# The maximum of a row of attention scores taken in two pieces and joined

## The chip, the cores and the metric

The kernel runs on one core of one Trainium2 chip. The metric is the device time of one execution in microseconds (us), as the median of three runs. Everything below about where the time lies comes from one profiled execution.

## What is computed

A two-layer diffusion backbone over 1024 latent tokens and 256 context tokens, width 1024, in fp32. Layer 0 mixes grouped-query attention with a convolution module, layer 1 a long convolution with a recurrence, and each is followed by a gated feed-forward net. The change lies in the attention of layer 0. It has 12 query heads over 4 key/value heads of width 64; latent queries attend to context and latent keys (1280 keys), context queries to the context alone (256 keys):

```python
def one_block(q_blk):
    s = jnp.einsum('bqhgd,bkhd->bhgqk', q_blk, k).astype(jnp.float32)
    p = jax.nn.softmax(s, axis=-1).astype(v.dtype)
    return jnp.einsum('bhgqk,bkhd->bqhgd', p, v)
...
attn_l = block_attention(q_l, jnp.concatenate([k_c, k_l], axis=1), jnp.concatenate([v_c, v_l], axis=1))
```

The softmax subtracts the maximum of each row of scores before the exponential. That maximum is what the change computes in another way.

## The kernel before

The kernel has stages that follow one another: the input projections, the attention stage (with what is left of the convolution module's LayerNorm beside it), the output projection, the feed-forward net, then layer 1. The attention stage is `attention_all`. It works through 4 groups (one key/value head each) of 15 units. A unit is one query head with 256 queries: 12 units of a group are latent queries with 1280 keys ("full units", 48 in all), 3 are context queries with 256 keys ("context units", 12 in all). A unit holds its 256 queries as two halves, i = 0 and i = 1, of 128 rows each.

`score_steps` makes the scores of a unit. All scores lie in one PSUM tile `S` of 2560 columns: columns 0 to 1023 hold half 0 against the latents, 1024 to 1279 half 0 against the context, 1280 to 1535 half 1 against the context, 1536 to 2559 half 1 against the latents. Every score is the sum of two matmuls (L1009 and L1010, the keys' rounded part and rest). For half 0 there are four matmuls of 512 columns and then four of 256, which are the context scores of both halves. For half 1 there are four of 512. Then VectorE takes the row maximum over all 1280 columns, negated, into `nm` (L1026), and ScalarE takes the exponential of the whole row with `nm` as bias and sums it (L1027: the exponential and, as a second instruction, the readout of the sum).

`value_steps` multiplies with the values: for each of five blocks of 256 keys TensorE transposes four tiles of `p` into the PSUM tile `pT` (L1049, two buffers), ScalarE copies it rounded to `ph` (L1053), VectorE puts the rest into `pl` (L1054, which frees the buffer of `pT`), and TensorE adds four products into `o` (L1060). At a unit's end TensorE spreads the reciprocal of the sums (L1067), ScalarE copies half of `o` to `bot` (L1068), and VectorE joins and scales the result `ot` (two instructions that show as L1189, a helper's line). The reciprocal `rs` (L1041) waits for both exponentials of its unit.

`attention_all` interleaves the steps of the score and value generators by a list of due times, and the scheduler of the tile framework then sets each engine's final order. Each engine works its own queue strictly in that order. Pools are made with `reuse_waits="tile"`.

Of the kernel before, what the change touches and what calls it, by code (L numbers as in the profile page):

```python
# [10 lines left out]
F32 = mybir.dt.float32  # L11
F32R = mybir.dt.float32r
AF = mybir.ActivationFunctionType
ALU = mybir.AluOpType
AX = mybir.AxisListType
PSUM = bass.MemoryType.PSUM

P = 128
# [4 lines left out]
T = TC + TL  # L23
# [224 lines left out]
class Kern:  # L248
# [750 lines left out]
    def score_steps(self, u, state):  # L999

        nc = self.nc
        ab, S = self.ab, self.S
        nk, r, o, h0 = u
        q, k1, k2, vs = self.gr[h0 // 3]
        at = ((0, TL), (T + TC, T))

        def mm(i, dst, key, n):
            a = q[:, r, o + i * P:o + i * P + P]
            nc.tensor.matmul(S[:, dst:dst + n], lhsT=a, rhs=k1[:, key:key + n], start=True, stop=False)  # L1009
            nc.tensor.matmul(S[:, dst:dst + n], lhsT=a, rhs=k2[:, key:key + n], start=False, stop=True)  # L1010
        nm, sm = (ab.tile([P, 2], F32, name=m, tag=m, bufs=4) for m in ("nm", "sm"))
        state["p"], state["sm"] = [], sm
        for i in range(2):
            lo = at[i][1]
            if nk == T:
                lo = min(at[i])
                for n in range(0, TL, 512):
                    mm(i, at[i][0] + n, TC + n, 512)
                    if n == 0:
                        yield  # L1020
            if i == 0:
                for n in range(2):
                    mm(n, at[n][1], 0, TC)
            s = S[:, lo:lo + nk]
            p = ab.tile([P, T], F32, name="p", tag="p", bufs=self.npr)[:, :nk]
            nc.vector.tensor_reduce(out=nm[:, i:i + 1], in_=s, op=ALU.max, axis=AX.X, negate=True)  # L1026
            nc.scalar.activation(p, s, AF.Exp, bias=nm[:, i:i + 1], accum_out=sm[:, i:i + 1])  # L1027
            state["p"].append(p)
            yield
# [921 lines left out]
```

## Time and profile before

| | us |
|---|---|
| runs | 3836.53, 3836.60, 3843.24 (median 3836.6) |
| the profiled execution | 3845.4, of which the span 3843.6 |
| attention stage in it | about 391 to 978, of it the first group to about 554 |
| TensorE busy in 554 to 687 (12 full and 3 context units) | 108.8 of 133 |
| VectorE busy there | 91.9 of 133 |
| ScalarE busy there | 84.3 of 133 |

The span runs from the first to the last instruction. Busy time of TensorE is that of its matmuls; their weight loads are a line of their own (PEld) and lie beside them. A row of the timeline gives the start in us from the span's start, the duration, engine, line, operation, output and inputs; brackets at its end give idle time of the engine just before it and what ended it. Rows of equal instructions are merged, with their count.

### The profile page before, as it was taken

To read this page: it belongs to the slowest core of one execution; us is meant where nothing else is said; L and a number is where in the kernel's file an instruction comes from. 1 tells how busy PE (TensorE), PEld (TensorE's weight loads), DVE (VectorE), ACT (ScalarE), POOL (GpSimd) and SP (SyncE) were. 2 spreads that over 40 slices of the span, in tenths; PEclk is the share of its full clock that TensorE was granted. 3 is DMA by queue.
4 is the path that set the end of the run, shared out by engine and by line. 5 is a ranking of instruction groups with operands and counts; after the bars stand their busy time and mean duration, and the time that the engine had idled before them with its cause. 6 is when DMAs were issued, how large, how long until landed. Compare 5 with 4: busy or idle time off the path is not lost.

```text
span 3843.6 us, 47920 instructions
## 1 busy us (share of the span) xinstructions
PE 3509.9 (91%) x18708; PEld 2920.9 (76%) x18708; DVE 2295.9 (60%) x2884; ACT 1237.7 (32%) x2115; POOL 1323.9 (34%) x964
## 2 busy tenths in 40 slices
PE   7988788888899999999999899999787899999998
PEld 4768567666787888888888778977666778888886
DVE  5987566667226656645556688365697453443435
ACT  4134666665233111222222422222112332222222
POOL 3248131110262111223333554356566642222223
PEclk9999799999999999999999999999888999999999
DMA  5374111000322223212222467522346311111111
GB/s 205 117 193 107 43 56 32 21 30 14 106 83 93 83 88 106 68 60 71 76 76 74 142 200 200 152 85 96 117 138 209 115 55 50 50 45 50 43 51 55
DMA packets 202866, 351.12 MB, mean 91 GB/s; under 512 B 23504, under 2 KB 124432, under 8 KB 202640
## 3 DMA queue, kind: packets, MB, share of 16 engines
q1 hardware_dynamic: 172240, 311.22, 25.0%
q0 software_dynamic: 26496, 30.48, 3.7%
q10 hardware_dynamic: 3904, 6.36, 0.5%
q8 instruction: 148, 2.42, 0.3%
q14 instruction: 78, 0.64, 0.1%
HBM read 275.04 MB, written 62.39 MB: 88 GB/s over the span
## 4 chain that ended last, share of the span: by engine, by line
PE 67%; DVE 12%; issue 4%; ACT 3%; DMA 2%; POOL 2%; SPq 0%; POOLq 0%; DVEq 0%; ACTq 0%
PE dl L338 13%; PE dl L339 13%; PE dl L340 13%; PE pj L338 2%; PE pj L340 2%; PE pj L339 2%; DVE nm L1026 2%; PE pT L1049 2%; PE o L1060 2%; DVE pl L1054 2%; PE S L1009 1%; PE dc L338 1%; PE dc L340 1%; PE dc L339 1%; PE S L1010 1%
## 5 line engine op out<-in xcount | busy, mean ns | idle before, releaser
L332 POOL TENSOR_TENSOR wlo<-wraw,whi 128x1024 fp32r<-128x1024 f32 (+1 forms) x226 | 579.1, 2568 | 1284.3 <-ACT whi L331 1273.6
L339 PE MATMUL dl<-hl,whi 128*128 128x512 f32 x1920 | 762.6, 397 | 3.9 <-POOL hl L1189 3.2
L338 PE MATMUL dl<-hh,whi 128*128 128x512 f32 x1536 | 606.9, 396 | 7.2 <-DVE fc L1100 4.0
L340 PE MATMUL dl<-hh,wlo 128*128 128x512 f32 x1536 | 608.0, 396 | 0.0
L331 ACT CAST whi<-wraw 128x1024 fp32r<-128x1024 f32 (+1 forms) x226 | 224.9, 1004 | 875.2 <-PE dl L339 401.7
L339 PEld LDWEIGHTS dl<-hl,whi 128*128 128x128 f32 x1920 | 362.4, 189 | 87.8 <-POOL hl L1189 4.8
L1098 DVE SCALAR_TENSOR_TENSOR fc<-dl,cols,fc 128x1023 f32<-128x1023 f32 x84 | 107.4, 1279 | 409.5 <-ACT fc L1097 409.4
L338 PEld LDWEIGHTS dl<-hh,whi 128*128 128x128 f32 x1536 | 289.3, 188 | 76.0 <-ACT nt L486 3.6
L340 PEld LDWEIGHTS dl<-hh,wlo 128*128 128x128 f32 x1536 | 289.5, 188 | 68.8
L872 DVE SCALAR_TENSOR_TENSOR x<-dl,modT,x 128x1024 f32<-128x1024 f32 x160 | 204.2, 1278 | 115.6 <-PE dl L340 114.1
L338 PE MATMUL dl<-gs,whi 128*128 128x512 f32 x640 | 253.3, 396 | 9.2 <-DVE fc L1100 9.2
L339 PE MATMUL dl<-gs,whi 128*128 128x512 f32 x640 | 250.2, 391 | 0.0
L340 PE MATMUL dl<-gs,wlo 128*128 128x512 f32 x640 | 249.8, 390 | 0.0
L1054 DVE TENSOR_TENSOR pl<-pT,ph 128x512 fp32r<-128x512 f32 x252 | 167.7, 686 | 67.5 <-ACT ph L1053 66.9
L1049 PE MATMUL pT<-ident,p 128*128 128x128 f32 x1008 | 166.0, 287 | 44.2 <-DVE pl L1054 37.3
L1053 ACT CAST ph<-pT 128x512 fp32r<-128x512 f32 x252 | 142.2, 587 | 150.1 <-PE pT L1049 148.4
L1026 DVE TENSOR_REDUCE nm<-S 128x1 f32<-128x1280 f32 (+1 forms) x120 | 153.0, 1275 | 49.5 <-PE S L1010 44.7
L1060 PE MATMUL o<-ph,vs 128*128 128x256 f32 x504 | 146.7, 304 | 34.9 <-ACT ph L1053 17.5
L1193 DVE SCALAR_TENSOR_TENSOR conv<-u,cols,conv 128x1287 f32<-128x1287 f32 (+14 forms) x104 | 173.2, 1695 | 0.9
L1049 PEld LDWEIGHTS pT<-ident,p 128*128 128x128 f32 x1008 | 120.7, 145 | 66.8 <-DVE pl L1054 51.2
L338 PE MATMUL dl<-hl,whi 128*128 128x512 f32 x384 | 154.0, 402 | 2.0 <-ACT whi L331 0.9
L1060 PE MATMUL o<-pl,vs 128*128 128x256 f32 x504 | 152.8, 326 | 2.1 <-DVE pl L1054 2.1
(376 smaller groups left out, 8340.6 us busy)
## 6 DMA issues: line engine op xcount, KB each, us to landing
wraw<-in_wup SPq DMA_DIRECT2D x88, 512.0 KB, 3.6
adaw<-in_adaw SPq DMA_DIRECT2D x128, 256.0 KB, 2.9
wraw<-in_wdn SPq DMA_DIRECT2D x44, 512.0 KB, 3.6
adaw<-in_adaw SPq DMA_DIRECT2D x32, 512.0 KB, 4.4
df<-in_dftf POOLq DMA_DIRECT2D x64, 256.0 KB, 3.9
wraw<-in_w1f SPq DMA_DIRECT2D x24, 512.0 KB, 3.8
x<-in_xT SPq DMA_DIRECT2D x16, 640.0 KB, 9.8
spd<-so SPq DMA_DIRECT2D x68, 128.0 KB, 2.6
```

The costliest lines, as they stand in the source:

```text
L331: nc.scalar.copy(hi[:, :cols], raw[:, :cols])
L332: nc.gpsimd.tensor_tensor(out=lo[:, :cols], in0=raw[:, :cols], in1=hi[:, :cols].bitcast(F32), op=ALU.subtract)
L338: mm(out, lhsT=lh, rhs=rh, start=first, stop=False)
L339: mm(out, lhsT=lh, rhs=rl, start=False, stop=False)
L340: mm(out, lhsT=ll, rhs=rh, start=False, stop=last)
L872: nc.vector.scalar_tensor_tensor(out=xl, in0=pl, scalar=self.mod(l, j, m, 0), in1=xl, op0=ALU.mult, op1=ALU.add)
L1026: nc.vector.tensor_reduce(out=nm[:, i:i + 1], in_=s, op=ALU.max, axis=AX.X, negate=True)
L1049: nc.tensor.transpose(pt[:, (2 * a + i) * P:(2 * a + i + 1) * P], p[:, kc * P:(kc + 1) * P], self.ident)
L1053: nc.scalar.copy(ph, pt)
L1054: nc.vector.tensor_tensor(out=pl, in0=pt, in1=ph.bitcast(F32), op=ALU.subtract)
L1060: nc.tensor.matmul(o, lhsT=vs[:, kc], rhs=x[:, a * 256:a * 256 + 256], start=(kc == 0 and j == 0), stop=(kc == nk // P - 1 and j == 1))
L1193: self.nc.vector.scalar_tensor_tensor(out=out, in0=a, scalar=s, in1=b, op0=ALU.mult, op1=op)
```

## The change

For a full unit the maximum is no longer one reduction over 1280 columns. As soon as the first 512 latent columns of a half have been issued, a first reduction is issued over what is there: columns 0 to 511 for half 0, and 1280 to 2047 (768 columns, the context scores and the first latents) for half 1. When the rest has been issued a second reduction takes the remaining columns: 768 for half 0, 512 for half 1. Both write into a small tile `mx`, negated, and the smaller of the two goes into `nm`. Context units keep their single reduction (now L1033). Nothing else is edited; lines after it shift by seven.

```diff
                 for n in range(0, TL, 512):
                     mm(i, at[i][0] + n, TC + n, 512)
                     if n == 0:
+                        e = at[i][0] + 512
+                        mx = ab.tile([P, 2], F32, name="mx", tag="mx", bufs=4)
+                        nc.vector.tensor_reduce(out=mx[:, 0:1], in_=S[:, lo:e], op=ALU.max, axis=AX.X, negate=True)
                         yield
...
-            nc.vector.tensor_reduce(out=nm[:, i:i + 1], in_=s, op=ALU.max, axis=AX.X, negate=True)
+            if nk == T:
+                nc.vector.tensor_reduce(out=mx[:, 1:2], in_=S[:, e:lo + nk], op=ALU.max, axis=AX.X, negate=True)
+                nc.vector.tensor_tensor(out=nm[:, i:i + 1], in0=mx[:, 0:1], in1=mx[:, 1:2], op=ALU.min)
+            else:
+                nc.vector.tensor_reduce(out=nm[:, i:i + 1], in_=s, op=ALU.max, axis=AX.X, negate=True)
```

The scheduler gives another order around it. TensorE before, from the end of one full unit in the last group to the first transposes of the next (`k` are the two parts of the keys, `p` the exponentials; the names in brackets are the engines' semaphores that a row waits for):

```order
L1067 MATMUL o<-ident,rs 64x128 x2
L1009 MATMUL S<-k_6739,q 128x512 [waits Activation_49]
L1010 MATMUL S<-k_6740,q 128x512
L1009 MATMUL S<-k_6739,q 128x512
L1010 MATMUL S<-k_6740,q 128x512
L1009 MATMUL S<-k_6739,q 128x256
L1010 MATMUL S<-k_6740,q 128x256
L1009 MATMUL S<-k_6739,q 128x256
L1010 MATMUL S<-k_6740,q 128x256
L1049 MATMUL pT<-ident,p 128x128 x6
```

All eight score matmuls stand together, and only the first of them waits, for ScalarE. TensorE now, at the same place of another unit of the same group (L1074 is the old L1067, L1056 the old L1049, L1067 the old L1060):

```order
L1074 MATMUL o<-ident,rs 64x128 x2
L1009 MATMUL S<-k_6892,q 128x512 [waits Activation_49]
L1010 MATMUL S<-k_6893,q 128x512
L1056 MATMUL pT<-ident,p 128x128 x6
L1009 MATMUL S<-k_6892,q 128x512 [waits DVE_49]
L1010 MATMUL S<-k_6893,q 128x512
L1009 MATMUL S<-k_6892,q 128x256
L1010 MATMUL S<-k_6893,q 128x256
L1009 MATMUL S<-k_6892,q 128x256
L1010 MATMUL S<-k_6893,q 128x256
L1067 MATMUL o<-ph,vs 128x256 [waits Activation_49]
```

The first pair of scores has moved ahead of the transposes, and the second pair now waits for VectorE. In the built program the value that it waits for is the one that the first reduction of the same half sets, in all 96 halves of full units: the second pair writes the tile `S` that this reduction reads, and the wait is put on the tile as a whole, though the columns are others.

VectorE before, from the first half of a full unit to the end of the unit (`nm` once for each half):

```order
L1026 TENSOR_REDUCE nm<-S 128x1 [waits PE_49]
L1054 TENSOR_TENSOR pl<-pT,ph 128x512 [waits Activation_49] x3
L1054 TENSOR_TENSOR pl<-pT,ph 128x512 [waits DVE_49,Activation_49]
L1026 TENSOR_REDUCE nm<-S 128x1 [waits PE_49]
L1054 TENSOR_TENSOR pl<-pT,ph 128x512 [waits DVE_49,Activation_49]
L1041 RECIPROCAL rs<-sm 128x2 [waits Activation_49]
L1189 TENSOR_TENSOR ot<-o,bot 64x256 [waits DMAHW6_49,Activation_49]
L1189 TENSOR_TENSOR ot<-o,ot 64x256 [waits DVE_49]
```

VectorE now, over one full unit of the same group (L1061 is the old L1054, L1196 the old L1189):

```order
L1022 TENSOR_REDUCE mx<-S 128x1 [waits PE_49]
L1061 TENSOR_TENSOR pl<-pT,ph 128x512 [waits Activation_49] x2
L1030 TENSOR_REDUCE mx<-S 128x1 [waits PE_49]
L1031 TENSOR_TENSOR nm<-mx 128x1 [waits DVE_49]
L1061 TENSOR_TENSOR pl<-pT,ph 128x512 [waits Activation_49] x2
L1022 TENSOR_REDUCE mx<-S 128x1 [waits PE_49]
L1061 TENSOR_TENSOR pl<-pT,ph 128x512 [waits Activation_49]
L1030 TENSOR_REDUCE mx<-S 128x1 [waits PE_49]
L1031 TENSOR_TENSOR nm<-mx 128x1 [waits DVE_49]
L1196 TENSOR_TENSOR ot<-o,bot 64x256 [waits DMAHW2_49,Activation_49]
L1196 TENSOR_TENSOR ot<-o,ot 64x256 [waits DVE_49]
```

Each reduction has become two, with subtractions `pl` between them, and a joining instruction that waits for the second. Counted over the program, in the first half the two reductions have two `pl` between them in 45 of 48 full units, and in 11 a `pl` also stands ahead of the join; in the second half a `pl` stands between the reductions in 24 units, and in 8 the first instruction of `ot` stands there and both `pl` ahead of the first reduction.

## Prediction

> **What bounds the kernel now.** I read the page first, for the engines and the chain that ended last, then the busy time by stretches of the attention stage, then the timeline of one unit in it. From the page, the busiest engine and the chain by engine:
>
> ```profile
> PE 3509.9 (91%) x18708; PEld 2920.9 (76%) x18708; DVE 2295.9 (60%) x2884; ACT 1237.7 (32%) x2115; POOL 1323.9 (34%) x964
> ...
> PE 67%; DVE 12%; issue 4%; ACT 3%; DMA 2%; POOL 2%; SPq 0%; POOLq 0%; DVEq 0%; ACTq 0%
> ```
>
> TensorE carries two thirds of the chain over the whole span, so what is worth asking is whether it carries the attention stage too. Busy time by stretches (columns as in the header):
>
> ```profile
> core 0: us, PE busy (x) PEld busy (x) DVE busy (x) ACT busy (x) POOL busy (x), PEclk, DMA share, GB/s
> 391.00:554.00 163.00, 126.80 (x683) 102.80 (x684) 87.51 (x143) 102.74 (x183) 49.30 (x92) 0.81 0.16 51
> 554.00:687.00 133.00, 108.84 (x737) 92.26 (x734) 91.94 (x138) 84.32 (x162) 24.28 (x50) 0.99 0.10 29
> ```
>
> The second stretch is one group of 12 full and 3 context units in 133 us. No engine is full in it: TensorE 108.84, VectorE 91.94, ScalarE 84.32, and the durations of matmuls overlap, which makes TensorE's figure too high. So the group is held by a chain of waits between engines. The timeline of one full unit shows it (start, duration, engine, line, operation):
>
> ```profile
> 886.62 0.33 PE L1049 MATMUL pT<-ident,p 128*128 128x128 f32 x1 [0.56 <-DVE pl L1054]
> 887.14 0.38 PE L1067 MATMUL o<-ident,rs 128*64 128x128 f32 x2
> 887.23 0.19 ACT L1027 ACTIVATION_READ_ACCUMULATOR p<-S,nm 128x1 f32 x1
> 887.47 0.50 PE L1009 MATMUL S<-k,q 128*128 128x512 f32 x1
> 887.56 0.37 ACT L1068 COPY bot<-o 64x256 f32<-64x256 f32 x1
> 887.81 0.40 PE L1010 MATMUL S<-k,q 128*128 128x512 f32 x1
> 887.96 0.42 DVE L1189 TENSOR_TENSOR ot<-o,bot 64x256 f32<-64x256 f32 x1 [0.34 <-ACT bot L1068]
> 888.05 0.40 PE L1009 MATMUL S<-k,q 128*128 128x512 f32 x1
> ...
> 888.88 0.28 PE L1010 MATMUL S<-k,q 128*128 128x256 f32 x1
> 889.00 0.82 PE L1049 MATMUL pT<-ident,p 128*128 128x128 f32 x6
> 889.20 1.49 DVE L1026 TENSOR_REDUCE nm<-S 128x1 f32<-128x1280 f32 x1 [0.36 <-PE S L1010]
> 889.58 1.07 ACT L1053 CAST ph<-pT 128x512 fp32r<-128x512 f32 x2 [1.65 <-PE pT L1049]
> 890.60 1.28 DVE L1054 TENSOR_TENSOR pl<-pT,ph 128x512 fp32r<-128x512 f32 x2
> 890.72 1.33 ACT L1027 ACTIVATE p<-S,nm 128x1280 f32<-128x1280 f32 x1
> 891.95 0.19 ACT L1027 ACTIVATION_READ_ACCUMULATOR p<-S,nm 128x1 f32 x1
> ...
> 893.10 0.39 PE L1009 MATMUL S<-k,q 128*128 128x512 f32 x1
> 893.62 0.69 DVE L1054 TENSOR_TENSOR pl<-pT,ph 128x512 fp32r<-128x512 f32 x1 [0.22 <-ACT ph L1053]
> 893.80 0.40 PE L1010 MATMUL S<-k,q 128*128 128x512 f32 x1
> 894.23 1.49 DVE L1026 TENSOR_REDUCE nm<-S 128x1 f32<-128x1280 f32 x1
> 895.64 0.68 DVE L1054 TENSOR_TENSOR pl<-pT,ph 128x512 fp32r<-128x512 f32 x1
> ...
> 896.98 0.20 ACT L1027 ACTIVATION_READ_ACCUMULATOR p<-S,nm 128x1 f32 x1
> 897.23 0.50 PE L1009 MATMUL S<-k,q 128*128 128x512 f32 x1
> ```
>
> Follow the scores. Half 0 starts at 887.47, 0.05 after the readout of the exponential before it ended (887.23 + 0.19 = 887.42). Its last matmul ends at 889.16, the maximum starts at 889.20 and takes 1.49, the exponential starts at 890.72, its readout ends at 892.14. Half 1 starts at 893.10, its maximum at 894.23, its readout ends at 897.18, and at 897.23 the next unit's half 0 starts. Counted from 887.42 that is a closed ring of 9.76 us: half 0 ends at 4.72, half 1 at 9.76. It is closed because the first scores of a half wait for the exponential of the other half, although they go to other columns: the waits are for `S` as a whole. The only slack in the ring is the 0.96 between 892.14 and 893.10, in which TensorE worked through transposes queued ahead of half 1.
>
> **What the change costs, part by part.** VectorE's prices, from the groups of the stretch 391 to 985 (the number behind the bar is busy time, then the mean in ns):
>
> ```profile
> L1054 DVE TENSOR_TENSOR pl<-pT,ph 128x512 fp32r<-128x512 f32 x252 | 167.7, 686 | 67.5 <-ACT ph L1053 66.9
> L1026 DVE TENSOR_REDUCE nm<-S 128x1 f32<-128x1280 f32 x96 | 143.1, 1490 | 45.0 <-PE S L1010 43.6
> ...
> L1026 DVE TENSOR_REDUCE nm<-S 128x1 f32<-128x256 f32 x24 | 9.9, 414 | 4.5 <-ACT p L1027 3.2 <-PE S L1010 1.1
> L1041 DVE RECIPROCAL rs<-sm 128x2 f32<-128x2 f32 x60 | 9.9, 165 | 38.2 <-ACT p L1027 38.1
> ```
>
> A reduction of 1280 columns takes 1.490, one of 256 takes 0.414: 1.05 ns a column and 0.145 besides. So 512 columns cost 0.68 and 768 cost 0.95, both between measured rows. The join of two columns isn't in the trace; the reciprocal on 128x2 (0.165) is its nearest row and the lower end, the 256 column reduction (0.414) the upper; I take 0.16, as it has even less to do. A half so costs 0.68 + 0.95 + 0.16 = 1.79 instead of 1.49, over 96 halves 29 us more on VectorE. That alone is no loss in time, since VectorE idles 41 of 133.
>
> [...]
>
> What matters is the ring. The edit means the first reduction to run in the shadow of the second pair of scores. But the second pair now waits for the first reduction (the wait for VectorE in the order, for the whole tile). So nothing is overlapped: first pair, first reduction, second pair, second reduction, join, exponential, one behind the other. Besides, VectorE has subtractions queued between the two reductions, and TensorE's queue stands still behind the waiting pair: the products `o`, the transposes behind them, and the result of the unit before.
>
> Half 0, counted as above from the readout's end at 0:
> - First pair 0.05 to 0.79: two matmuls of 512 took 0.74 from start to end (887.47 to 887.81 + 0.40).
> - First reduction, 512 columns: 0.82 to 1.50.
> - Second pair and context scores: 1.55 to 2.76. In the trace such six took 1.11 (888.05 to 889.16); 0.10 more as they start from a stop, like the first one at 887.47.
> - Meanwhile six transposes go out at 0.63 (0.58 after the first matmul, as at 888.05). The copies `ph` start 0.58 after such transposes (889.00 to 889.58), so 1.21; the first is done at 1.80, and the pair of `pl` runs 1.82 to 3.10 (1.28, as at 890.60). It stands ahead of the second reduction, which could have started at 2.79.
> - Second reduction, 768 columns: 3.12 to 4.07. Join: 4.10 to 4.26. Exponential with readout, 1.42 (890.72 to 892.14): 4.29 to 5.71. Before: 4.72. Loss 0.99.
>
> Half 1:
> - First pair 5.76 to 6.50. The fourth `ph` is queued behind the exponential, 5.73 to 6.32, so its `pl` (0.69, as at 893.62), which stands ahead of the reduction, runs 6.34 to 7.03.
> - First reduction, 768 columns: 7.05 to 8.00. Second pair: 8.05 to 8.79. The last `pl` 8.02 to 8.71.
> - Second reduction, 512 columns: 8.82 to 9.50. Join 9.53 to 9.69.
> - The exponential stands behind the copy `bot` on ScalarE. `bot` waits for TensorE's last products, which wait for the last `pl`: from there to the end of L1067 is 0.90 (886.62 to 887.14 + 0.38), so 8.75 to 9.65, and `bot` (0.37) 9.69 to 10.06.
> - Exponential 10.08 to 11.51. The ring takes 11.51 instead of 9.76: a loss of 1.75 for a full unit; the old slack of 0.96 is eaten in it.
>
> In 8 units both `pl` stand ahead of the first reduction of half 1 and the first `ot` between the reductions: first reduction 7.76 to 8.71, second pair to 9.50; `ot` waits for `bot`, but by then has it (9.11 to 9.53); second reduction 9.55 to 10.23, second `ot` (0.42, as at 887.96) to 10.67, join to 10.86, exponential to 12.32. That is 0.81 more. In 11 units a `pl` of 0.69 stands ahead of the join of half 0.
>
> The sum: 48 x 1.75 + 8 x 0.81 + 11 x 0.69 = 84.0 + 6.5 + 7.6 = 98.1 us. The first group (163 us in the stretches above, other work in between) and the 12 full units beside context units are counted like the rest. What follows attention starts when it has ended, so the loss goes through: the profiled execution's 3845.4 would be 3943.5, and against the median of the runs, 3836.6, the forecast is 3934.7.
>
> **Rivals.**
> - *The wait doesn't hold anything up, and the change works as meant.* Then half 0 keeps its scores, and behind the last of them stand 0.95 + 0.03 + 0.16 = 1.14 instead of 1.49; half 1 has 0.87 instead of 1.49. That is 0.97 a unit or 47 us: 3790. It decides where the first reduction ends before TensorE reaches the second pair. For it: six transposes (0.66) stand between the pairs. Against: they are too short to cover 0.03 + 0.68 + 0.05, and in half 1 the reduction lasts 0.95 and starts late. Chance 0.06. [...]
> - *Only the bare ring grows*, because the subtractions give way (copies come earlier than I time them). Half 0: second reduction 2.80 to 3.75, exponential to 5.39, so 0.67 lost; half 1: pairs and reductions back to back, exponential 8.88 to 10.31. Loss 0.55 a unit, 26 us: 3863. For it: idle VectorE; against it the order, in which `pl` stands ahead in nearly every unit. Chance 0.14.
> - *The queues jam further*: every unit loses the 2.56 of the slowest kind, 123 us: 3960. It decides where `pl` generally comes later than the scores in half 1. Chance 0.10.
>
> The forecast itself has 0.70.
>
> **Range and chances.** The range takes in the bare ring and the jam: 3862 to 3965. The join's upper end would add 96 x 0.25 = 24 us, which the upper end nearly holds. About 0.2% (8 us) is what runs of this kernel can tell apart, as the three shown spread over 7. Only the first rival is faster; a little of the bare ring could fall within 0.2%. Faster 0.06, same 0.02, slower 0.92.
>
> **What would show it.** In the profile after: 192 reductions with mean near 0.82 in place of 96 of 1.49, and joins near 0.16; score matmuls idle for VectorE's `mx`, which no row shows now; a full unit in 11 to 12 us instead of 9.7, and the stage some 98 longer; TensorE's and ScalarE's busy time unchanged. Wrong if the second pairs start right behind the first, or if units keep their 9.7.

## The result, and the profile after

The changed kernel takes 3960.97 us (median of four runs, 3959.93 to 3961.32), the kernel before 3839.92 beside it (four runs, 3836.53 to 3847.43): a ratio of 1.0311, 95% interval 1.0297 to 1.0325. It is slower by 121 us where 98 were forecast. Two executions that ran far longer than the others of their kernel, one in the experiment with half 0 alone (5000.89) and one of the kernel before (8284.92), are left out of the medians and ratios below. The profiled execution after has a span of 3958.7 against 3843.6. Its page, engines and chain:

```profile
PE 3579.3 (90%) x18708; PEld 2963.9 (75%) x18708; DVE 2332.0 (59%) x3076; ACT 1238.3 (31%) x2113; POOL 1321.3 (33%) x964
...
PE 67%; DVE 11%; ACT 6%; issue 3%; DMA 2%; POOL 2%; SPq 0%; ACTq 0%; DVEq 0%; POOLq 0%
```

Read two numbers here. VectorE has 36 us more work (2332.0 against 2295.9), as the split must give. TensorE has 69 us more (3579.3 against 3509.9) with the same 18708 matmuls, which no edit gives: the same matmuls kept it busy for longer. The stretches of the attention stage, cut where the reciprocal `rs` of every fifteenth unit starts, so by groups of 15 units (columns as in the prediction's header; the granted clock is the third number from the end, and 1.00 is full speed):

```profile
391.00:600.00 209.00, 155.93 (x807) 123.95 (x807) 113.21 (x218) 116.41 (x210) 53.29 (x99) 0.80 0.15 46
...
600.00:761.00 161.00, 125.14 (x741) 101.71 (x742) 100.41 (x186) 85.79 (x163) 25.54 (x52) 0.91 0.09 25
761.00:925.00 164.00, 127.89 (x741) 104.90 (x740) 100.19 (x186) 84.92 (x159) 11.97 (x24) 0.87 0.05 11
925.00:1089.00 164.00, 125.84 (x691) 103.10 (x690) 101.05 (x186) 79.22 (x141) 7.10 (x3) 0.84 0.08 22
```

A group that took 133 (at a granted clock of 0.99 in the prediction's row) takes 161 to 164 at 0.84 to 0.91. The stage, which ended at 976 before, ends at 1089: 113 of the span's 115 are lost in it. VectorE's groups in the stage, and TensorE's scores of 512 columns:

```profile
L1061 DVE TENSOR_TENSOR pl<-pT,ph 128x512 fp32r<-128x512 f32 x252 | 170.5, 689 | 105.4 <-ACT ph L1060 104.1
L1030 DVE TENSOR_REDUCE mx<-S 128x1 f32<-128x768 f32 x48 | 45.8, 955 | 10.2 <-PE S L1010 9.4
...
L1022 DVE TENSOR_REDUCE mx<-S 128x1 f32<-128x512 f32 x48 | 33.1, 690 | 27.3 <-PE S L1010 27.3
...
L1031 DVE TENSOR_TENSOR nm<-mx 128x1 f32<-128x1 f32 x96 | 20.8, 217 | 2.4
...
L1009 PE MATMUL S<-k,q 128*128 128x512 f32 x192 | 105.3, 548 | 101.5 <-ACT p L1034 85.3 <-DVE mx L1022 12.7
```

The same scores before:

```profile
L1009 PE MATMUL S<-k,q 128*128 128x512 f32 x192 | 87.3, 454 | 22.8 <-ACT p L1027 22.7
```

The reductions cost 0.69 and 0.95, as priced. The two rows of the scores show how such a wait is read. The wait that the change added, for `mx`, has only 12.7 us of TensorE's idle time to its name, since the transposes in front of it fill most of it. Far more idle time has come at another wait: 85.3 for the exponential `p`, where 22.7 stood before, at the point where a unit's scores close the ring. The first experiment shows that most of this too comes from the new wait.

One unit, and the start of the next, to be laid beside the forecast's steps (start, duration, engine, line, operation):

```profile
1033.49 0.19 ACT L1034 ACTIVATION_READ_ACCUMULATOR p<-S,nm 128x1 f32 x1
...
1033.74 0.50 PE L1009 MATMUL S<-k,q 128*128 128x512 f32 x1 [1.90 <-ACT p L1034]
...
1034.50 0.69 DVE L1022 TENSOR_REDUCE mx<-S 128x1 f32<-128x512 f32 x1 [0.62 <-PE S L1010]
...
1035.25 0.50 PE L1009 MATMUL S<-k,q 128*128 128x512 f32 x1
1035.50 1.29 DVE L1061 TENSOR_TENSOR pl<-pT,ph 128x512 fp32r<-128x512 f32 x2 [0.31 <-ACT ph L1060]
...
1036.70 0.95 DVE L1030 TENSOR_REDUCE mx<-S 128x1 f32<-128x768 f32 x1
...
1037.72 0.69 DVE L1061 TENSOR_TENSOR pl<-pT,ph 128x512 fp32r<-128x512 f32 x1
...
1038.33 0.15 DVE L1031 TENSOR_TENSOR nm<-mx 128x1 f32<-128x1 f32 x1
...
1039.98 0.50 PE L1009 MATMUL S<-k,q 128*128 128x512 f32 x1
...
1041.05 0.95 DVE L1022 TENSOR_REDUCE mx<-S 128x1 f32<-128x768 f32 x1
...
1042.05 0.50 PE L1009 MATMUL S<-k,q 128*128 128x512 f32 x1
...
1042.12 0.37 ACT L1075 COPY bot<-o 64x256 f32<-64x256 f32 x1 [1.71 <-PE o L1074]
...
1042.52 0.42 DVE L1196 TENSOR_TENSOR ot<-o,bot 64x256 f32<-64x256 f32 x1 [0.53 <-ACT bot L1075]
1042.86 0.67 DVE L1030 TENSOR_REDUCE mx<-S 128x1 f32<-128x512 f32 x1
1043.46 0.41 DVE L1196 TENSOR_TENSOR ot<-o,ot 64x256 f32<-64x256 f32 x1
1043.79 0.14 DVE L1031 TENSOR_TENSOR nm<-mx 128x1 f32<-128x1 f32 x1
1043.97 1.33 ACT L1034 ACTIVATE p<-S,nm 128x1280 f32<-128x1280 f32 x1 [1.48 <-DVE nm L1031]
...
1045.44 0.50 PE L1009 MATMUL S<-k,q 128*128 128x512 f32 x1 [2.65 <-ACT p L1034]
...
1046.95 0.79 PE L1009 MATMUL S<-k,q 128*128 128x512 f32 x1
```

Everything stands in series: first pair, reduction (1034.50), second pair at 1035.25 just after it, the two `pl` ahead of the second reduction, a `pl` ahead of the join, the exponential. In half 1 the second pair again starts (1042.05) behind the first reduction (1041.05 + 0.95), and what stands around the second reduction are the two instructions of `ot`. From 1033.74 to 1045.44 the unit takes 11.70. The last two rows show what the forecast doesn't have. TensorE stood idle for 2.65 before 1045.44, and in the next unit the second pair's first matmul takes 0.79 instead of 0.50. By stretches: the 3.41 us around the idle time, the 3.41 us behind them, then this unit, the next one and an earlier one:

```profile
1043.31:1046.72 3.41, 1.28 (x8) 1.01 (x8) 1.31 (x5) 1.55 (x3) 0.00 (x0) 1.00 0.09 19
1046.72:1050.13 3.41, 3.28 (x14) 2.99 (x14) 2.50 (x5) 0.94 (x2) 0.00 (x0) 0.50 0.00 0
1033.74:1045.44 11.70, 8.60 (x55) 6.75 (x55) 7.43 (x15) 5.84 (x10) 0.00 (x0) 1.00 0.06 13
1045.44:1057.66 12.22, 9.93 (x54) 7.97 (x54) 7.79 (x15) 5.72 (x10) 0.00 (x0) 0.86 0.00 0
924.56:937.42 12.86, 10.83 (x54) 9.15 (x54) 7.84 (x15) 5.88 (x11) 0.00 (x0) 0.76 0.25 82
```

The clock granted from 1046.72 to 1050.13 is 0.50. The unit at full clock takes 11.70, the next one 12.22 at 0.86, the earlier one 12.86 at 0.76.

### The profile page after: what moved, and what is told of

Same layout as the page of the kernel before. It is cut to its first block, busy times and chain, and to the rows that moved or that the text cites. A ratio compares the mean times of both kernels' runs of the same rounds, so it can differ in the third digit from the quotient of the medians.

```text
span 3958.7 us, 48014 instructions
## 1 busy us (share of the span) xinstructions
PE 3579.3 (90%) x18708; PEld 2963.9 (75%) x18708; DVE 2332.0 (59%) x3076; ACT 1238.3 (31%) x2113; POOL 1321.3 (33%) x964
## 4 chain that ended last, share of the span: by engine, by line
PE 67%; DVE 11%; ACT 6%; issue 3%; DMA 2%; POOL 2%; SPq 0%; ACTq 0%; DVEq 0%; POOLq 0%
PE dl L338 13%; PE dl L339 13%; PE dl L340 13%; ACT p L1034 3%; PE pT L1056 2%; PE S L1009 2%; PE pj L338 2%; PE pj L340 2%; PE pj L339 2%; PE o L1067 1%; PE S L1010 1%; PE dc L338 1%; PE dc L340 1%; PE dc L339 1%; DVE pl L1061 1%
## 5 line engine op out<-in xcount | busy, mean ns | idle before, releaser
L339 PE MATMUL dl<-hl,whi 128*128 128x512 f32 x1920 | 764.2, 398 | 3.8 <-POOL hl L1196 2.8
L1009 PE MATMUL S<-k,q 128*128 128x512 f32 (+1 forms) x312 | 145.9, 472 | 123.5 <-ACT p L1034 107.3
L1061 DVE TENSOR_TENSOR pl<-pT,ph 128x512 fp32r<-128x512 f32 x252 | 170.5, 689 | 105.4 <-ACT ph L1060 104.1
L1056 PE MATMUL pT<-ident,p 128*128 128x128 f32 x1008 | 190.8, 319 | 19.3 <-DVE pl L1061 8.7
L1060 ACT CAST ph<-pT 128x512 fp32r<-128x512 f32 x252 | 143.2, 587 | 170.7 <-PE pT L1056 168.5
L1009 PEld LDWEIGHTS S<-k,q 128*128 128x128 f32 x312 | 71.7, 230 | 162.4 <-ACT p L1034 127.6
L1056 PEld LDWEIGHTS pT<-ident,p 128*128 128x128 f32 x1008 | 143.0, 164 | 54.9 <-DVE pl L1061 23.6
L1067 PE MATMUL o<-pl,vs 128*128 128x256 f32 x504 | 161.9, 341 | 1.5 <-DVE pl L1061 1.4
L1067 PE MATMUL o<-ph,vs 128*128 128x256 f32 x504 | 150.8, 311 | 10.2 <-ACT ph L1060 4.9
```

The source lines that it names most:

```text
L339: mm(out, lhsT=lh, rhs=rl, start=False, stop=False)
L1056: nc.tensor.transpose(pt[:, (2 * a + i) * P:(2 * a + i + 1) * P], p[:, kc * P:(kc + 1) * P], self.ident)
L1060: nc.scalar.copy(ph, pt)
L1061: nc.vector.tensor_tensor(out=pl, in0=pt, in1=ph.bitcast(F32), op=ALU.subtract)
L1067: nc.tensor.matmul(o, lhsT=vs[:, kc], rhs=x[:, a * 256:a * 256 + 256], start=(kc == 0 and j == 0), stop=(kc == nk // P - 1 and j == 1))
```

## Experiments

**The wait taken away.** The second pair of scores no longer waits for the first reduction; it goes to columns that this reduction doesn't read (`first` holds the reduction). All work is as in the changed kernel; TensorE's order is that of before again, with all score matmuls of a half together.

```diff
-            nc.tensor.matmul(S[:, dst:dst + n], lhsT=a, rhs=k1[:, key:key + n], start=True, stop=False)
-            nc.tensor.matmul(S[:, dst:dst + n], lhsT=a, rhs=k2[:, key:key + n], start=False, stop=True)
+            for m in (nc.tensor.matmul(S[:, dst:dst + n], lhsT=a, rhs=k1[:, key:key + n], start=True, stop=False),
+                      nc.tensor.matmul(S[:, dst:dst + n], lhsT=a, rhs=k2[:, key:key + n], start=False, stop=True)):
+                if first:
+                    self.tc.declare_no_dep(m.ins, first[-1].ins, reason="other columns, other banks")
```

> The changed kernel, with one thing undone: the second pair of score matmuls no longer waits for the first reduction of its half (the two touch other columns of the score tile, and the dependence between them is declared void). TensorE's order is then that of before again; the three VectorE instructions of each half stay. Theory (the loss comes from the wait): nearly all of the 121 us goes, 3840 to 3870, and no score matmul is idle for a reduction. Rival (the loss comes from what VectorE's queue now holds: three instructions in place of one, with a subtraction between the second reduction and the join in most halves): worked along this kernel's order as in the prediction, a full unit takes about 11.3 us, so 3915, and over 3900 in any case.

Measured: 3866.39 against 3843.60 beside it, ratio 1.0062 (1.0043 to 1.0081). So about 95 of the 121 us are gone. The second group in its profile:

```profile
586.00:725.00 139.00, 112.61 (x741) 94.33 (x739) 94.95 (x185) 84.07 (x162) 25.33 (x52) 0.98 0.10 29
```

And its row of the scores of 512 columns among TensorE's groups:

```profile
L1009 PE MATMUL S<-k,q 128*128 128x512 f32 x192 | 88.6, 461 | 33.5 <-ACT p L1038 33.4
```

The group is down to 139, the idle time before the scores falls from 101.5 to 33.5, and the clock is 0.98. The wait, with the order that the scheduler makes around it, is the cause of most of the loss; the 23 us that stay aren't the wait's.

**The wait without the work.** The single reduction of before, and in place of the first of the two a useless one over 2 columns (its result is not used), which the second pair then waits for.

```diff
-                        nc.vector.tensor_reduce(out=mx[:, 0:1], in_=S[:, lo:e], op=ALU.max, axis=AX.X, negate=True)
+                        nc.vector.tensor_reduce(out=mx[:, 0:1], in_=S[:, lo:lo + 2], op=ALU.max, axis=AX.X, negate=True)
...
-                nc.vector.tensor_reduce(out=mx[:, 1:2], in_=S[:, e:lo + nk], op=ALU.max, axis=AX.X, negate=True)
-                nc.vector.tensor_tensor(out=nm[:, i:i + 1], in0=mx[:, 0:1], in1=mx[:, 1:2], op=ALU.min)
...
+            nc.vector.tensor_reduce(out=nm[:, i:i + 1], in_=s, op=ALU.max, axis=AX.X, negate=True)
```

> The kernel before, its single reduction over 1280 columns kept, with one useless reduction over two columns put where the change puts its first one (its result is not used). So the wait of the second pair is there, but VectorE does only some 0.15 us more in each half. Theory (the wait): the ring of a full unit goes through the stop and the two subtractions ahead of the full reduction, 11.3 us in place of 9.76, 48 x 1.5 = 74 us more: 3913. Rival (VectorE's additional work): 96 x 0.17 = 16 us at most, 3856.

Measured: 3971.97, ratio 1.0336 (1.0314 to 1.0357): slower than the change itself, and by 128 us where some 74 were expected. The rows of the scores of 512 columns and of the useless reduction:

```profile
L1009 PE MATMUL S<-k,q 128*128 128x512 f32 x192 | 105.6, 550 | 93.9 <-ACT p L1029 91.3 <-DVE mx L1021 2.3
...
L1021 DVE TENSOR_REDUCE mx<-S 128x1 f32<-128x2 f32 x96 | 14.8, 154 | 42.5 <-PE S L1010 42.5
```

An instruction of 0.154 us, 96 times (14.8 us of work), costs 128 us once the second pair waits for it. The direction is shown; the size was missed, and is taken up below.

**The split without the early start.** Both reductions and the join after all scores of the half; there is then no wait between the pairs.

```diff
-                        nc.vector.tensor_reduce(out=mx[:, 0:1], in_=S[:, lo:e], op=ALU.max, axis=AX.X, negate=True)
...
+                nc.vector.tensor_reduce(out=mx[:, 0:1], in_=S[:, lo:e], op=ALU.max, axis=AX.X, negate=True)
                 nc.vector.tensor_reduce(out=mx[:, 1:2], in_=S[:, e:lo + nk], op=ALU.max, axis=AX.X, negate=True)
```

> The changed kernel with both reductions issued after all scores of a half, so that no score matmul waits for one; the three VectorE instructions stay. Theory (the wait): the ring grows by 0.33 for a half, 48 x 0.66 = 32 us, 3870. Rival (VectorE's queue): in this kernel's order one or two subtractions stand between the second reduction and the join, 0.69 each, so 1.2 to 1.8 us a unit, 3895 to 3925.

Measured: 3921.9, ratio 1.0207 (1.0182 to 1.0233). My theory of 32 us was wrong, the rival right. VectorE's rows of one half show why:

```profile
804.68 0.95 DVE L1029 TENSOR_REDUCE mx<-S 128x1 f32<-128x768 f32 x1
805.55 0.68 DVE L1030 TENSOR_REDUCE mx<-S 128x1 f32<-128x512 f32 x1
806.14 0.68 DVE L1061 TENSOR_TENSOR pl<-pT,ph 128x512 fp32r<-128x512 f32 x1
806.74 0.15 DVE L1031 TENSOR_TENSOR nm<-mx 128x1 f32<-128x1 f32 x1
```

The second reduction ends at 806.23, but the join of 0.15 stands behind a subtraction and starts at 806.74. An operation cut into three leaves room in VectorE's queue for others, on the path that the exponential waits for. How much of the 78 us that is was not measured by itself: the stage's granted clock fell here too, to 0.89 from 0.93 before (0.93 without the wait), and some of the 78 may be the clock's. Together with the first experiment: without the wait, starting the first reduction early gains 55 us over starting it late (3866 against 3922). The idea of the change does work, but the split costs more than the idea gains, and the wait comes on top.

**The halves apart.** The change for half 0 alone, and for half 1 alone (the other half keeps its single reduction). The edit for half 0; for half 1 it says `i == 1`.

```diff
-                        nc.vector.tensor_reduce(out=mx[:, 0:1], in_=S[:, lo:e], op=ALU.max, axis=AX.X, negate=True)
+                        if i == 0:
+                            nc.vector.tensor_reduce(out=mx[:, 0:1], in_=S[:, lo:e], op=ALU.max, axis=AX.X, negate=True)
...
-            if nk == T:
+            if nk == T and i == 0:
```

> The change made for half 0 alone; half 1 keeps its single reduction over 1280 columns. Theory (each stop of TensorE at a reduction lengthens the ring, with the subtractions that stand ahead): half 0 ends 0.99 later, half 1 gives nothing back, so about 0.95 to 1.2 us for a full unit and 46 to 58 us in all, 3885 to 3900. Rival (the loss is in VectorE's additional instructions, 0.30 for a half): 48 x 0.30 = 14 us, 3854.

> The change made for half 1 alone; half 0 keeps its single reduction. Theory: with half 0 as before, half 1's first reduction stands behind the fourth subtraction (ends at 7.9 in a unit's time), the second pair behind that, the copy of the result ahead of the exponential, which ends at 11.35 instead of 9.76: 1.6 us a unit, 76 us, 3915 to 3930. Together with half 0's loss that would be the whole of the 121. Rival (VectorE's additional instructions): 14 us, 3854.

Measured: half 0 alone 3877.92, ratio 1.009 (1.0057 to 1.0123), some 34 us where the steps gave 46 to 58; half 1 alone 3914.25, ratio 1.0175 (1.015 to 1.0201), 70 us where they gave 76. Each half loses, half 1 about twice as much. Together they give 0.0265 of the 0.0311.

**Half 1 alone, without its wait.** The edits of the last one and of the first one together.

> The change made for half 1 alone and its second pair of scores freed of the wait. Beside the same kernel with the wait (half 1 only) it shows what the wait costs there. Theory (the wait): back to within 25 us of the kernel before, 3835 to 3865. Rival (VectorE's queue, where a subtraction stands ahead of the join): 1.1 us a unit, 3893.

Measured: 3857.4, ratio 1.0034 (1.0018 to 1.0049). The wait alone is 57 us of half 1's 70.

**Where the waits of before could go.** The forecast says that before was bound by waits for the whole of `S`. So in the kernel before, the latent scores of one half were freed from waiting for the other half's maximum and exponential (other columns), first for half 1, as below, then for half 0 (`i == 0`). `readers` holds that maximum and exponential.

```diff
+                if n == 512 and i == 1:
+                    for x in self.readers[1 - i]:
+                        self.tc.declare_no_dep(m.ins, x.ins, reason="other columns, other banks")
```

> The kernel before, without the change. The four latent score matmuls of half 1 no longer wait for the maximum and the exponential of half 0 of the same unit (other columns; the dependence is declared void). It asks whether the ring of waits through the whole score tile is what bounds a full unit. If it is: half 1's scores and most of half 0's chain overlap, the ring is 0.05 + 1.7 + 1.5 + 1.4 (half 0) + 1.5 + 1.4 (half 1, whose maximum waits for half 0's exponential) = 7.6 us in place of 9.76, and VectorE's 7.4 us of work in a unit is close behind: up to 48 x 2 = 96 us less, 3745 to 3800. If a unit is bound by VectorE, TensorE and ScalarE taking turns whatever the scores wait for: 3830 to 3845.

> The kernel before, without the change; the latent scores of half 0 no longer wait for the maximum and exponential of half 1 of the unit before (other columns). If the ring through the score tile is all that bounds a unit, 0.95 to 1.2 us a unit go, 3783 to 3795. If VectorE's and TensorE's queues bound it as soon as the ring is a little shorter (as freeing half 1 has shown): 3835 to 3870.

Measured: half 1 freed 3865.99, ratio 1.0065 (1.005 to 1.008), slower, where both theories were missed. Half 0 freed 3834.07, ratio 0.9973 (0.996 to 0.9986): a gain of about 10 us, just beyond the 3835 to 3870 of the queues' theory and far from the ring's 50 us. It is the only version here that beats both kernels. For the slower one, its maximum's row which also names the waits:

```profile
L1030 DVE TENSOR_REDUCE nm<-S 128x1 f32<-128x1280 f32 x96 | 143.1, 1491 | 103.5 <-PE S L1010 54.0 <-ACT p L1031 49.0
```

The maximum now idles 103.5 us at the head of VectorE's queue where it idled 45.0 before, 49.0 of it for ScalarE's exponential: the scores came earlier, but their maximum has a wait for the other half's exponential too, and the subtractions stand behind it. (The stage's granted clock was 0.90 against 0.93 before, so some of the 22 us may be the clock's.) So a wait that is taken away uncovers the next one close behind. What puts that wait there was not tried; `nm` is one tile for both halves, which half 0's exponential reads and half 1's maximum writes.

**TensorE kept busy.** What was open is the 23 us above the forecast, and the lower clock. In the changed kernel 14 useless transposes were put ahead of a full unit's first scores, into columns of `S` that are overwritten right behind. They wait for the second reduction of the half before, not for the exponential, and so fill the time in which TensorE idled. The second kernel has the same in the one with the useless reduction.

```diff
+        if nk == T and self.exps:
+            for j in range(14):
+                m = nc.tensor.transpose(S[:, (j % 4) * P:(j % 4 + 1) * P], self.ident, self.ident)
+                self.tc.declare_no_dep(m.ins, self.exps[-1].ins, reason="other columns, other banks")
         for i in range(2):
```

> The changed kernel with 14 useless transposes of 128x128 (some 1.6 us at 0.11 each) put into TensorE's queue ahead of the first scores of each full unit, into columns of S that are overwritten right behind; they wait for the second half's second reduction, not for the exponential, and so mostly fill the 2.6 us in which TensorE now idles before a unit. In 30 of 47 units they stand right ahead of the first pair. Theory: the part of the loss above the forecast, some 20 us, is TensorE's granted clock, which falls because of that idling; kept busy, the stage's clock goes from about 0.87 to 0.95 or more, units go to about 11.7, and the time is 3935 to 3952 in spite of the added work. Rival: the clock has nothing to do with the idling; then the time is 3961 or more, as the transposes only add work (up to 10 us more where they stand elsewhere).

> The same 14 useless transposes in the kernel that has the single reduction of before and a useless reduction of 2 columns for the wait (measured at 3971.97). In 21 of 47 units they stand right ahead of the first pair. Theory (the clock falls by idling): 3935 to 3960 with a clock in the stage some 0.04 to 0.08 higher. Rival (no link): 3972 or more with the same clock.

Measured: 3939.94, ratio 1.0251 (1.0228 to 1.0273), against the change's 1.0311 (1.0297 to 1.0325); and 3939.51, ratio 1.0255 (1.0232 to 1.0277), against 1.0336 (1.0314 to 1.0357). Both are faster, by 21 and 32 us, for having 658 matmuls more. From the first one's profile, the second to fourth group:

```profile
588.00:750.00 162.00, 140.26 (x911) 115.49 (x908) 98.77 (x186) 85.97 (x165) 25.66 (x52) 0.95 0.09 26
750.00:907.00 157.00, 136.66 (x908) 112.93 (x908) 97.98 (x186) 84.50 (x159) 12.02 (x24) 0.97 0.05 11
907.00:1066.00 159.00, 131.88 (x848) 108.26 (x847) 98.73 (x187) 79.79 (x143) 7.10 (x3) 0.96 0.08 24
```

And the transposes at the end of one unit in its timeline:

```profile
1022.72 1.75 PE L1015 MATMUL S<-ident 128*128 128x128 f32 x14 [0.81 <-DVE mx L1034]
...
1024.57 0.50 PE L1009 MATMUL S<-k,q 128*128 128x512 f32 x1
```

They end at 1024.47 and hold nothing up: the first scores start at 1024.57, after the exponential. The clock in these groups, 0.84 to 0.91 in the changed kernel, is 0.95 to 0.97, and the groups go from 161, 164 and 164 to 162, 157 and 159. Over the whole stage the granted clock was 0.93 before, 0.85 in the changed kernel and in the one with the useless reduction, and is 0.94 in both with the transposes: what the clock had lost is back. The rival, that idling and clock have no link, falls: it asked for 3961 and 3972 or more. One reserve stays: the transposes also change where some instructions stand in TensorE's queue; in 17 of 47 units they don't stand right ahead of the scores (in 26 of the second kernel).

## Why the prediction was right, and what it missed

- **The ring and the wait**: right. Without the wait about 95 of 121 us are gone, the wait put into the kernel before costs as much as the change, and in the timeline the second pair starts 0.06 after the first reduction's end (1034.50 + 0.69, then 1035.25).
- **The prices on VectorE**: 0.68, 0.95 and 0.16 were taken; 0.69, 0.95 and 0.217 were measured. The change adds 36.1 us of work there where 29 were worked out, the join being dearer in the mean than the 0.15 it takes in the unit shown. For a half the rows give (45.8 + 45.7 + 33.1 + 32.9 + 20.8) / 96 - 1.49 = 0.37 more, where my row sum had 0.30, which is low mostly by the join. (The second 768 row, 45.7, and the second 512 row, 32.9, are not shown.)
- **That the split itself is no loss** ("that alone is no loss in time, since VectorE idles 41 of 133"): wrong. With nothing early and no wait it costs 78 us, some of it perhaps through the clock. Idle time in the mean is no cover: the added instructions stand at the point that the exponential waits for, and let a subtraction in ahead of the join. The sum by the unit's steps had these queue positions in it, so the forecast didn't suffer.
- **The unit**: 98.1 over 48 full units is a mean of 2.04 more, so 9.76 + 2.04 = 11.80. The last three groups have nine full units at full clock that lead straight into another full unit; they take 10.87 to 12.44, 11.57 in the mean. For single units the steps are less exact, and that the mean fits is in part luck. The unit shown has a subtraction ahead of the join of half 0, and the first `ot` between the reductions of half 1, so the sum gives it both extras: 11.51 + 0.69 + 0.81 = 13.01. It took 11.70. Half 0 came out near (1039.93 - 1033.68 = 6.25, where the steps give 5.71 + 0.69 = 6.40). But the extras don't add up: with one subtraction already done ahead of the join, one fewer was left to run ahead of half 1's first reduction, which started at 1041.05 - 1033.68 = 7.37, where the steps with both extras have 7.76 + 0.69 = 8.45.
- **The ring as what bounds the kernel before**: shown only in part. That more work in it lengthens a unit is shown. But with either half's scores freed, the kernel gained 10 us or lost 22, so engines' queues and further waits stand close behind the ring.
- **"TensorE's and ScalarE's busy time unchanged"**: this is where the size went wrong. ScalarE's is (1238.3 against 1237.7), TensorE's isn't, 69 us up. Some 26 of them need no slower clock: at full clock TensorE is busy for 8.60 in the unit shown and for 8.06 in the prediction's unit (887.47 to 897.23), and 48 x 0.54 = 26, as a 512 column matmul that starts from a stop shows 0.50 here (1033.74) and one behind another 0.40 (887.81 before). The rest can be the clock's. A sum of durations from before takes matmuls at before's clock of 0.99. The longer ring has TensorE idle for more of the time (36 of 161 us in the second group, 24 of 133 before), the clock falls to 0.50 for a time after it (3.41 us from 1046.72), and slow matmuls lie in the ring (0.79 at 1046.95). That term, missing from the sum, is about 21 us, by the experiment that keeps TensorE busy: with it the change costs 96 us beside the forecast's 98.
- **Not all of that is exact.** In the last three groups the forecast's share is 74 us. The change lost 90 there (489 against 400, between the reciprocals of the fifteenth and the last unit), the busy kernel 78. In the first group it is the other way round: forecast 25, change 23, busy kernel 12; there the clock was low before as well (0.81 in the prediction's row), so that the transposes can also win back what before lost.
- **Rivals.** "The queues jam further" gave 3960, the time that came, but not by its way: it asked for units of 12.3 from queue positions, and the nine units at full clock take 11.57 in the mean. That its number came is luck. "Works as meant" (3790) falls twice: the wait holds, and without it the time is still 3866. Whether the second pairs have to wait at all, a time can't show; the first reductions took the same without the wait (0.684 and 0.951 in the mean) as with it (0.690 and 0.951). The 3790 was out of reach even so, as the split's own cost stood against it.
- **Open**: the useless reduction's 128 us. With TensorE kept busy 95.5 are left, where I had worked out 74; 21 are not explained.

## What to carry to other kernels

Before an operation is started early on part of a tile, look at what the program makes the writers of the rest wait for: here dependences are kept by the whole tile, and an instruction of 0.15 us that reads two columns of it, 96 times, cost 128 us. Cutting an operation on the critical path into pieces cost more here than the pieces (78 us where 32 were worked out), as others got into the queue between them. And where a change made TensorE wait longer, its matmuls' durations from the trace of before no longer held (548 ns in the mean for 512 columns of scores, not 454): read the granted clock with them.

## What was not expected of the hardware

The clock did not fall in the idle time itself. After the 2.65 us ahead of 1045.44 it stayed at 1.00 for 1.28 us of matmuls and was then 0.50 from 1046.72 to 1050.13, for 3.41 us. In that stretch a 512 column matmul took 0.79 instead of 0.50. The next two stretches at 0.50 lasted 3.42 (1060.37 to 1063.79) and 10.24 (1070.61 to 1080.85), one and three times as long, and all their edges lie a whole number of 3.41 us apart. So the changed kernel's attention stage can be cut into pieces of 3.41 us along these edges, and each piece has one clock:

| TensorE busy in a piece at full clock | pieces | next piece at 0.50 |
|---|---|---|
| under 1.5 us | 18 | 18 |
| 1.5 to 1.9 us | 22 | 17 |
| over 1.9 us | 104 | 2 |

From 0.50 the clock came back behind 32 of the 33 pieces in which TensorE was busy for more than 3.2 us, and behind 5 of the other 27. So in this stage a piece with TensorE busy for less than about half of it has mostly cost the clock of the next one (35 of the 40 pieces under 1.9 us, 2 of the 104 above), though matmuls ran in it: 1.28 us of them in the one from 1043.31 to 1046.72. The same gap can thus cost nothing or much, by where the edges lie. One of 1.90 us ahead of 1033.74 is split by the edge at 1033.07, TensorE is busy for 2.12 and 2.61 in the two pieces, and the clock stays at 1.00; one of 1.90 ahead of 1057.66 ends in a piece with 1.96, and the fall at 1060.37 follows. Filling the gap with 14 useless transposes won 21 us back.
